# One step of a hybrid layer: the HGRN2 heads run inside the z phase, the gate product in the output stage

## The chip, the cores and the metric

The kernel runs on one core of a Trainium2 chip. The metric is device microseconds of one execution. Engines are named as in the profile: PE is TensorE (PEld its weight loads), DVE VectorE, ACT ScalarE, POOL GpSimd, SP the engine that issues most loads.

## What is computed

One layer of a streaming encoder on 512 prompt frames and 32 sample frames, which share all weights (T = 544 columns, kept transposed: channels on partitions).

```python
mod = silu(c) @ w_ada + b_ada                     # shift, scale, gate
h = rmsnorm(x) * (1 + scale) + shift
z = h @ w_in                                      # 2048 x 15360
au, av, ag, lx, lg, hq, hf, hi, hg, mg = split(z)
ya = gelu(au) * spatial_mix(rmsnorm(gelu(av))) * silu(ag)      # gMLP, 8 groups
yb = rglru(causal_conv(lx)) * silu(lg)                         # RG-LRU, 8 blocks
yc = rmsnorm(hgrn2(silu(hq), hf, hi)) * silu(hg)               # HGRN2, 8 heads
ga, gb, gc = split(sigmoid(mg))
out = (ga * (ya @ wb0) + gb * (yb @ wb1) + gc * (yc @ wb2)) @ w_out
y = rmsnorm(x + gate * out)
```

HGRN2 is a gated recurrence, worked out per head in chunks of 64 with decay factors for blocks of 1, 2, 4, 8, 16, 32 frames.

## The kernel before

Each large product is taken in about full fp32 precision as three reduced ones: a weight tile is split on chip into a rounded part `wh` (ACT copy) and a rest `wl` (DVE subtraction), in `split` and `halved`, and `rows3` multiplies `wh` with both parts of the operand and `wl` with the first.

The program is one list of *items* (`items`), each with a `prep` (split the weights of this item), a `mul` (its products) and a `post` (evict). The loop at the end emits, for item i: the loads that are due, `prep` of item i+2 (`AHEAD = 2`), `mul` of i, `post` of i, and one call of `pump()`. This emission order is the order of every engine's queue; an engine never passes a waiting instruction. Four stages follow each other:

- *Start*: 64 items that make shift and scale, beside the norm of x.
- *z phase*: 60 groups (`Group`), each makes two blocks of 128 channels of z with a Strassen-like scheme of 7 items; an item is 24 products of 128x128 by 128x272. Per group four weight tiles go through the ring `raw` (`RAWS` buffers of 512 KB) and one through the ring `q`; one of the `raw` tiles and the `q` tile get a second tile added in flight, by an accumulating DMA that POOL issues once the first has landed (`load_adds`, L267). `z_groups` sets the order of the groups: 4 of `av`, the light ones (heads' inputs hf, hq, hi, hg and the merge gates mg, whose results are spilled to DRAM), the 16 heavy ones (gMLP and RG-LRU) with light ones between. The small work of a gMLP group or an RG-LRU block is a generator (`gm_gen`, `lru_gen`) that `pump` advances by one step per item.
- *Merges*: `ya @ wb0` and `yb @ wb1` (16 blocks each of 48 products), then `yc @ wb2` in two passes of 16 half blocks (`part`). While they run, `pump` advances the 8 head generators (`hg_gen`), two at a time in turn, also between the parts of an item (`cuts`). The operands of the z phase are closed by then, and heads live in an arena of their own (`harena`, 46 units).
- *Output*: 16 blocks of `w_out` (two items of 48 products each), the residual and the last norm.

The gate product (`gate_item`, 32 items of 4 products whose stationary operand has 2 columns, through the ring `raw`) is spread over z groups 5 to 12, four to a group.

Of the kernel before, what the change touches and what calls it, by code (L numbers as in the profile page):

```python
# [13 lines left out]
NP = 512  # L14
# [28 lines left out]
RAWS = 6  # L43
# [63 lines left out]
def hybrid_step_kernel(ctx: ExitStack, tc: tile.TileContext, xT, cT, w_first, w_in, w_branch, w_out,  # L107
# [56 lines left out]

    arenas = {}
# [4 lines left out]
    def hbuf(n=T):  # L170
        try:
            return Buf(arenas["h"], n)
        except MemoryError:
            return Buf(arenas["a"], n)
# [134 lines left out]
    def halved(src, width=1024):  # L309

        wh = wp.tile([128, 1024], F32R, tag="wh", name="wh", bufs=3)
        wl = wp.tile([128, 1024], F32R, tag="wl", name="wl", bufs=3)
        split(wh[:, :width], wl[:, :width], src[:, :width])
        return wh, wl

    def rows3(p, w, rhs, kt, start, stop, **kw):

        wh, wl = w
        n = len(kt)
        for i, k in enumerate(kt):  # L320
            s = slice(i * 128, (i + 1) * 128)
            for q, (a, r) in enumerate(((wh, 0), (wh, 1), (wl, 0))):
                mm(p, a[:, s], rhs(k, r), start=start and i == 0 and q == 0,  # L323
                   stop=stop and i == n - 1 and q == 2, **kw)
# [78 lines left out]
    def plain_item(src, kt, rhs, p, first, last, post=None, pre=None, hs=(0, 1), cuts=(4,)):  # L403
# [8 lines left out]
        def mul():  # L412
            w = c.pop("w")
            n = len(kt)
            for lo, hi in zip((0, *cuts), (*cuts, n)):
                for h in hs:
                    rows3(pms[p][:, h, :HF], [a[:, lo * 128:hi * 128] for a in w], lambda k, r: rhs(k, r, h), kt[lo:hi],
# [14 lines left out]
    MIX = ((6, 5), (7, 3))  # L432

    def o_block(j, post, pre, hs):
        p = turn["p"] % 2
        turn["p"] += 1
        for z in range(2):
            plain_item(w_out[j, :, 8 * z:8 * z + 8, :].rearrange("p k n -> p (k n)"), range(8),
                       lambda k, r, h, z=z: X[MIX[z][h]][:, k, r, :], p, z == 0, z == 1,
                       (lambda: post(pms[p])) if z else None, None if z else pre, hs)  # L440

# [6 lines left out]
    heads = {"next": 8, "run": []}  # L448

    def pump():  # L450
# [39 lines left out]
    def square_x(q):  # L490
        if q == 0:
            st["xss"] = po()
        act(st["sq"][q % 2], st["x"][q], AF.Square)

    def sum_x(q):
        for i in range(2):
            for h in range(2):
                mm(st["xss"][:, 512 * h:512 * h + HF], ones, st["sq"][q % 2][:, i, h * HF:(h + 1) * HF],
                   start=q == 0 and i == 0, stop=q == 7 and i == 1)

    def rstd_x():
# [36 lines left out]
    def sums(c):  # L538
# [15 lines left out]
        put(4, c, hi)  # L554

    def start_items():
        for c in range(8):
            for part in range(2):
                for q in range(4):
# [18 lines left out]
                    def post(c=c, n=n):  # L578
# [13 lines left out]
                        if n == 3 and c == 4:  # L592
                            pools.close("early")
                            pools.close("scratch")
                            operand(pools.open("x4", "right"), 4)
                        if n == 7:
                            ada_post(c)
                            if c == 7:
# [5 lines left out]
                                operand(pools.open("x3", "right"), 3)  # L604
                                for i in range(4, 8):
                                    put(3, i, st["x"][i][:, :, :HF])
# [6 lines left out]
    NUNIT = 27  # L613
# [91 lines left out]
    def hg_setup():  # L705

        hg["x"] = hbuf(len(LEVELS) * XW)
# [3 lines left out]
        hg["A"] = [hbuf(SLOT) for _ in range(2)]  # L711
        for a in hg["A"]:
            nc.gpsimd.memset(a.ap, 0.0)
        t = hbuf(len(LEVELS) * 256)
        nc.gpsimd.dma_start(out=t.ap, in_=consts[:, 130:130 + len(LEVELS) * 256])
        nc.vector.tensor_copy(hg["masks"].rearrange("p a e n -> p (a e n)"), t.ap)
# [11 lines left out]
    def hg_gen(h):  # L728
        cell = {}
        zf, zi, zg = (hbuf() for _ in range(3))  # L730

        a = next(a for a in (arenas["h"], arenas["a"]) if a.pairs() > 1)
        kq = [Buf(a, T), Buf(a, T + 1)]
        kb, qb = sorted(kq, key=lambda b: b.col)
        kb.ap, qb.ap = kb.ap[:, :T], fv(qb.ap, 0, [[1, T + 1]])
        for b, n in ((zf.ap, "hf"), (qb.ap[:, 1:], "hq"), (zi.ap, "hi"), (zg.ap, "hg")):
            nc.gpsimd.dma_start(out=b, in_=scratch[f"{n} {h}"])
        nc.gpsimd.memset(qb.ap[:, 0:1], 0.0)
        if h == 0:
            hg_setup()  # L740
            for _ in range(3):
                yield
        yield
        lb, l1, ln1 = (lbt[:, i, h:h + 1] for i in range(1, 4))
        t1, t2, g = hbuf(), hbuf(), hbuf()
        act(t1.ap, zf.ap, AF.Abs)
        ts(g.ap, zf.ap, 0.0, None, op0=OP.min)
        act(t2.ap, zf.ap, AF.Relu)
# [13 lines left out]
        zf.free()  # L762
        cell.update(q=True, v=zi, hg=zg)
# [10 lines left out]

        def lev(m):
            if m not in LEVELS:
                return w32["b"].ap, 0
            i = LEVELS.index(m)
            return hg["x"].ap[:, i * XW:(i + 1) * XW], 128
# [29 lines left out]
        A = hg["A"][h % 2].ap  # L809
# [13 lines left out]
        def lev_put(m, p):  # L823
            i = LEVELS.index(m)
            for r, e, lo, n, half, src in ((128, 0, 0, 256, 1, 128), (128, 1, AO, 256, 0, 0),
# [3 lines left out]
                    o, hg["masks"][:r, i, e, :n // 2].rearrange("p (b m) -> p b m", m=m),  # L829
                    p[:r, src:src + n // 2].rearrange("p (b m) -> p b m", m=m))  # L830

        while "busy" in hg:
            yield
        hg["busy"] = h
# [3 lines left out]
        lev_w(1)  # L838
        lev_e(16)
        lev_e(8)  # L840
        lev_d(4)
        lev_d(2)
# [3 lines left out]
        p1 = lev_mm(1)  # L846
        lev_e(4)
        lev_e(2)
        lev_put(1, p1)
        lev_w(4)  # L850
        lev_w(2)
        lev_d(32)
# [5 lines left out]
        p1, p2 = lev_mm(16), lev_mm(8)  # L858
        lev_e(32)
        act(ke.ap, ke.ap, AF.Exp)  # L860
        eq, qe = hbuf(T + 1), hbuf(T + 1)
        nc.gpsimd.memset(eq.ap[:, 0:1], 0.0)
        act(eq.ap[:, 1:], g64.ap, AF.Exp)
        lev_put(16, p1)
        lev_put(8, p2)
# [10 lines left out]
        p1, p2 = lev_mm(4), lev_mm(2)  # L876
        mm(p1[:NS, 272:273], ke.ap[:, NP:], qb.ap[:, T:T + 1], start=True, stop=True)
        nc.vector.tensor_copy(A[:NS, AS + NS:AS + NS + 1], p1[:NS, 272:273])
        lev_put(4, p1)
        lev_put(2, p2)  # L880
        g32.free()
        g64.free()
        hg.pop("busy")
# [21 lines left out]
        for w in range(4):  # L905
            nc.tensor.transpose(pv[:, w * 128:(w + 1) * 128], cell["v"].ap[:, w * 128:(w + 1) * 128], ident)
# [14 lines left out]
        nc.tensor.transpose(pq[:NS, :128], cell["v"].ap[:, NP:], ident)  # L921
# [7 lines left out]
        cell["v"].free()  # L929
# [553 lines left out]
```

## Time and profile before

| | |
|---|---|
| median of 3 runs | 2284.67 us (2283.12 to 2287.73) |
| the profiled execution | 2280.29 us, span 2278.6 us |
| mean granted clock of PE | 0.953 |
| PE busy | 2058.2 us (90%), 15864 records |
| DVE, ACT, POOL busy | 1245.4, 995.2, 520.6 us |

The span is read by stages: start to 117.6 us, z phase to 1580 us, merges to 2070 us, output to 2262.5 us, and a tail to 2278.6 us. Within the z phase the gate items stand at 250 to 521 us, the gMLP groups mostly in 500 to 960 us, the RG-LRU blocks in 960 to 1580 us. PE, the engine with the most work, has matmuls that overlap each other, so its pace is read from how many of them a stretch holds. PEclk is the granted share of its full clock.

### The profile page before, as it was taken

What the parts mean: (1) busy time and instruction counts of PE and PEld (TensorE: products, weight loads), DVE (VectorE), ACT (ScalarE), POOL (GpSimd) and SP (SyncE); (2) the same over time, 40 slices, a digit from 0 to 9 for tenths busy, and PEclk for the clock granted to TensorE, in tenths of its full rate; (3) what the DMA queues carried; (4) which work ended last, traced back from release to release, by engine and by line L of the source; (5) the groups of instructions that cost most, each with busy time, mean ns of one, the idle gap of its engine ahead of it and who ended that gap; (6) DMA issues with size and microseconds to landing.
All of it is one profiled execution on the core that took longest, in us unless ns stands there. A gap on an engine that the chain in (4) does not pass through costs nothing. (4 is left out here: it accounts for less than half of the span.)

```text
span 2278.6 us, 39024 instructions
## 1 busy us (share of the span) xinstructions
PE 2058.2 (90%) x15864; PEld 1954.0 (86%) x15864; DVE 1245.4 (55%) x1729; ACT 995.2 (44%) x1616; POOL 520.6 (23%) x737
## 2 busy tenths in 40 slices
PE   5789878779999999999999999998798898979997
PEld 3279767669999999989999999998787888878997
DVE  3455434336666666566666666655655556443235
ACT  3455422224444444446464546544544444323233
POOL 0011110011121212111212111113645556322112
PEclk8789998899999999999999999999898999999999
DMA  8976575667677777766767676777343544765333
GB/s 326 374 186 173 163 205 175 181 201 207 186 208 190 194 199 199 195 165 174 191 168 194 174 188 180 201 197 236 128 148 115 146 121 111 183 207 172 113 113 125
DMA packets 139605, 416.57 MB, mean 183 GB/s; under 512 B 16641, under 2 KB 38945, under 8 KB 139425
## 3 DMA queue, kind: packets, MB, share of 16 engines
q1 hardware_dynamic: 89712, 261.08, 34.1%
q0 software_dynamic: 43728, 142.80, 27.8%
q10 hardware_dynamic: 5984, 10.19, 1.4%
q8 instruction: 125, 2.05, 0.4%
q14 instruction: 56, 0.45, 0.1%
HBM read 366.00 MB, written 48.01 MB: 182 GB/s over the span
## 5 line engine op out<-in xcount | busy, mean ns | idle before, releaser
L323 PE MATMUL pm<-x,wh 128*128 128x272 f32 x6720 | 1303.2, 293 | 72.3 <-ACT wh L188 48.7
L323 PEld LDWEIGHTS pm<-x,wh 128*128 128x128 f32 x6720 | 1081.0, 193 | 93.5 <-ACT wh L188 53.1
L323 PE MATMUL pm<-x,wl 128*128 128x272 f32 x3360 | 984.7, 293 | 6.7 <-DVE wl L233 6.7
L323 PEld LDWEIGHTS pm<-x,wl 128*128 128x128 f32 x3360 | 644.3, 192 | 11.3 <-DVE wl L233 11.1
L233 DVE TENSOR_TENSOR wl<-raw,wh 128x1024 fp32r<-128x1024 f32 (+1 forms) x342 | 408.1, 1194 | 330.0 <-ACT wh L188 329.2
L323 PE MATMUL pp<-x,wh 128*128 128x272 f32 x2048 | 415.2, 301 | 25.0 <-DVE arena L1205 23.2
L188 ACT ACTIVATE wh<-raw 128x1024 fp32r<-128x1024 f32 (+1 forms) x342 | 342.0, 1012 | 165.8 <-PE pm L323 88.3
L323 PEld LDWEIGHTS pp<-x,wh 128*128 128x128 f32 x2048 | 336.4, 198 | 32.6 <-issue 23.2
L233 DVE TENSOR_TENSOR wl<-q,wh 128x1024 fp32r<-128x1024 f32 x180 | 220.1, 1223 | 258.5 <-ACT wh L188 258.4
L323 PE MATMUL pp<-x,wl 128*128 128x272 f32 x1024 | 303.7, 297 | 1.1 <-DVE wl L233 1.1
L188 ACT ACTIVATE arena<-pm 128x272 f32<-128x272 f32 x240 | 94.5, 394 | 457.7 <-PE pm L323 446.1
L267 POOL DMA_DIRECT2D q<-in_w_in_dram x60 | 53.0, 883 | 737.6 <-DMA q<-in_w_in_dram 508.8
L188 ACT ACTIVATE wh<-q 128x1024 fp32r<-128x1024 f32 x180 | 189.3, 1052 | 66.9 <-DMA q<-in_w_in_dram 65.5
L323 PEld LDWEIGHTS pp<-x,wl 128*128 128x128 f32 x1024 | 201.5, 197 | 1.3 <-DVE wl L233 1.3
L188 ACT ACTIVATE arena<-arena 128x544 f32<-128x544 f32 (+3 forms) x166 | 90.6, 562 | 197.9 <-DVE arena L394 89.6
L364 DVE TENSOR_TENSOR q<-q,raw 128x1024 f32<-128x1024 f32 x120 | 147.1, 1226 | 4.1
L188 ACT ACTIVATE harena<-harena 128x272 f32<-128x272 f32 (+3 forms) x134 | 63.3, 532 | 74.1 <-DVE harena L766 21.7
L267 POOL DMA_DIRECT2D raw<-in_w_in_dram x60 | 54.1, 901 | 129.9 <-DMA raw<-in_w_in_dram 104.1
L1205 DVE TENSOR_TENSOR arena<-pp,arena 128x544 f32<-128x544 f32 x64 | 46.1, 720 | 50.7 <-DMA arena<-d_mg 27.7
L188 ACT ACT_TABLE_LOAD x44 | 56.5, 1283 | 13.6 <-DVE arena L1049 8.2
L791 POOL TENSOR_TENSOR harena<-harena 128x544 f32<-128x544 f32 (+1 forms) x39 | 54.7, 1424 | 1.4 <-DVE harena L806 1.3
L1209 POOL DMA_DIRECT2D d_mix<-arena x32 | 28.4, 888 | 91.2 <-DVE arena L1205 70.9
(332 smaller groups left out, 1785.2 us busy)
## 6 DMA issues: line engine op xcount, KB each, us to landing
raw<-in_w_in_dram SPq DMA_DIRECT2D x240, 512.0 KB, 5.5
q<-in_w_in_dram SPq DMA_DIRECT2D x60, 512.0 KB, 4.3
q<-in_w_in_dram POOLq DMA_DIRECT2D x60, 512.0 KB, 6.2
raw<-in_w_in_dram POOLq DMA_DIRECT2D x60, 512.0 KB, 7.4
raw<-in_w_ss_dram SPq DMA_DIRECT2D x44, 512.0 KB, 8.2
raw<-in_w_out_dram SPq DMA_DIRECT2D x38, 512.0 KB, 4.0
raw<-in_w_gate_dram SPq DMA_DIRECT2D x32, 512.0 KB, 5.4
raw<-in_w_branch_dram SPq DMA_DIRECT2D x32, 512.0 KB, 3.9
```

Of the source, the lines that this page charges most:

```text
L188: return nc.scalar.activation(out, in_, func, **kw)
L233: tt(lo, src, hi.bitcast(F32), op=OP.subtract)
L267: nc.gpsimd.dma_start(out=raws[n], in_=src, accum_op=OP.add)
L323: mm(p, a[:, s], rhs(k, r), start=start and i == 0 and q == 0, stop=stop and i == n - 1 and q == 2, **kw)
L364: tt(raws[n], raws[n], raws[m], op=OP.add)
L791: ptt(v, fv(src, 0, [[2 * m, nb], [m - 1, 2], [1, m]]), fv(src, m - 1, [[2 * m, nb], [0, 2], [0, m]]), op=OP.subtract)
L1205: tt(two(g.ap), halves(p), two(g.ap), op=OP.mult)
L1209: nc.gpsimd.dma_start(out=scratch[f"mix {j}"], in_=g.ap, accum_op=OP.add)
```

## The change

- *Heads in the z phase.* One head at a time, started when its four inputs are spilled (`heads["ready"]`); `pump` leaves out every third call for them. The order of groups is now 4 of `av`, then a head's group and a light one in turn (four groups and 28 items per head), 3 light, and the 16 heavy with one light one after every fourth. Heads use the common arena (32 units instead of 27, none of their own). The levels run in another order: 16 and 8 first, 1 last, with one step more between a level's factors and its products; only two factor buffers are kept, and `hi` and `hg` are loaded where they are used. The result is spilled (`y2`) and read back.
- *Smaller buffers.* `RAWS` is 5 instead of 6; `wh` and `wl` are five tiles of 512 instead of three of 1024, so each split is two instructions; PSUM has four banks `px` instead of two `px` and a pair `po`.
- *Gate product* in the output stage: 28 of its 32 items follow one `w_out` item each, the first four stand in the last merge.
- *Third branch* in one pass of 16 whole blocks; the mixed rows go to operands 1, 2, 6, 5. The convolution of RG-LRU has one step more.

```diff
@@ sizes and rings
-RAWS = 6
+RAWS = 5
-    NUNIT = 27
+    NUNIT = 32
-        return ps.tile([128, 512], F32, tag="x", name="px", bufs=2)
-    def po():
-        return ps.tile([128, 1024], F32, tag="o", name="po", bufs=1)
+        return ps.tile([128, 512], F32, tag="x", name="px", bufs=4)
@@ halved
-        wh = wp.tile([128, 1024], F32R, tag="wh", name="wh", bufs=3)
-        wl = wp.tile([128, 1024], F32R, tag="wl", name="wl", bufs=3)
-        split(wh[:, :width], wl[:, :width], src[:, :width])
-        return wh, wl
+        got = []
+        for o in range(0, width, 512):
+            wh = wp.tile([128, 512], F32R, tag="wh", name="wh", bufs=5)
+            wl = wp.tile([128, 512], F32R, tag="wl", name="wl", bufs=5)
+            split(wh, wl, src[:, o:o + 512])
+            got += [(wh[:, i:i + 128], wl[:, i:i + 128]) for i in range(0, 512, 128)]
+        return got
@@ pump
-        run = heads["run"]
-        while len(run) < 2 and heads["next"] < 8:
-            run.append(hg_gen(heads["next"]))
+        heads["tick"] += 1
+        if heads["tick"] % 3 == 0:
+            return
+        if heads["run"] is None and heads["next"] < heads["ready"]:
+            heads["run"] = hg_gen(heads["next"])
             heads["next"] += 1
-        if run:
-            g = run.pop(0)
-            if next(g, "end") != "end":
-                run.append(g)
+        if heads["run"] is not None and next(heads["run"], "end") == "end":
+            heads["run"] = None
@@ hg_gen
-        zf, zi, zg = (hbuf() for _ in range(3))
+        if h == 0:
+            hg_setup()
+        zf = hbuf()
...
-        while "busy" in hg:
-            yield
-        hg["busy"] = h
         lev_d(16)
         lev_d(8)
         yield
-        lev_w(1)
         lev_e(16)
         lev_e(8)
+        lev_w(16)
+        lev_w(8)
+        yield
+        p1, p2 = lev_mm(16), lev_mm(8)
+        yield
+        lev_put(16, p1)
+        lev_put(8, p2)
         lev_d(4)
         lev_d(2)
...
+        nc.gpsimd.dma_start(out=spill(f"y2 {h}"), in_=g)
@@ z_groups
-        todo += light[:10]
-        rest = iter(light[10:])
+        todo = av
+        for i in range(16):
+            todo += [head[i], light[i]]
+        todo += light[16:19]
+        rest = iter(light[19:])
         for i, (b1, b2, post, at_start) in enumerate(heavy):
             todo.append((b1, b2, post, {1: at_start}))
-            todo += [next(rest) for _ in range(1 + i % 2)]
+            if i % 4 == 3:
+                todo.append(next(rest))
...
-                if i in (2, 6, 5, 3) and 5 <= n < 13:
-                    gate_item(n - 5, (2, 6, 5, 3).index(i))
@@ merges
-        merge(1, 1, (6, 5), None, on1)
-        merge(2, 2, (1, 2), 0, wait(4))
-        merge(3, 2, (1, 2), 1, wait(9))
+        merge(1, 1, (6, 5))
+        merge(2, 2, (7, 3))
@@ out_items
+        def gate_next(j):
+            def f(z):
+                if j // 2 < 7:
+                    gate_item(j // 2 + 1, 2 * (j % 2) + z)
+            return f
-            o_block(j, post_j(j, (0, 1)), pre(j), (0, 1))
+            o_block(j, post_j(j, (0, 1)), pre(j), (0, 1), gate_next(j))
```

Three places of the engines' queues, before and after. The first is POOL in the z phase, between two groups that make head inputs; `raw` and `q` rows are the accumulating loads, `d_...` rows spills. Before:

```order
L1119 DMA d_hq_6_3661<-arena_820 128x544
L267 DMA raw_3566<-in_w_in_dram 128x1024
L267 DMA q_3701<-in_w_in_dram 128x1024
L1119 DMA d_hf_7_3912<-arena_820 128x544
L1119 DMA d_hq_7_3916<-arena_820 128x544
L267 DMA raw_3821<-in_w_in_dram 128x1024
L267 DMA q_3956<-in_w_in_dram 128x1024
```

After, where head 1 begins; L751 and L757 are the two sums of its gates, L765 and L788 the sums behind its scan and the factors of levels 16 and 8:

```order
L738 DMA arena_826<-d_hf_1_3401 128x544
L738 DMA arena_826<-d_hq_1_3405 128x544
L739 MEMSET arena_826 128x1
L751 TENSOR_TENSOR arena_826<-arena_826 128x544
L757 TENSOR_TENSOR arena_826<-arena_826 128x544
L765 TENSOR_TENSOR arena_826<-arena_826 128x8x32
L788 TENSOR_TENSOR arena_826<-arena_826 128x17x2x16
L788 TENSOR_TENSOR arena_826<-arena_826 128x34x2x8
L266 DMA raw_4087<-in_w_in_dram 128x1024
L266 DMA q_4202<-in_w_in_dram 128x1024
```

The two accumulating loads now stand behind eight instructions of a head.

The second is ACT at the gate step of a head (`hg_gen`, from Abs to the second Ln). Before, in the merges, the split in `wh` being that of one 48-product item:

```order
L188 ACTIVATE harena_15147<-harena_15147 128x34x8 x2
L188 ACTIVATE harena_15147<-harena_15147 128x544 x3
L188 ACTIVATE harena_15147<-harena_15147,cv_75 128x544
L188 ACTIVATE harena_15147<-harena_15147,lbt_80 128x544
L188 ACTIVATE harena_15147<-harena_15147 128x544
L188 ACTIVATE harena_15147<-harena_15147,lbt_80 128x544
L188 ACTIVATE wh_15386<-raw_14993 128x1024
```

After, in the z phase, `pm` rows being evictions of z items:

```order
L190 ACTIVATE wh_4078<-q_3926 128x512
L190 ACTIVATE wh_4082<-q_3926 128x512
L190 ACTIVATE arena_826<-pm0_115 128x272
L190 ACTIVATE arena_826<-arena_826 128x544 x2
L194 ACT_TABLE_LOAD
L190 ACTIVATE arena_826<-arena_826 128x544
L190 ACTIVATE arena_826<-arena_826,cv_75 128x544
L190 ACTIVATE arena_826<-arena_826,lbt_80 128x544
L190 ACTIVATE arena_826<-arena_826 128x544
L190 ACTIVATE arena_826<-arena_826,lbt_80 128x544
L190 ACTIVATE wh_4129<-raw_3849 128x512
L190 ACTIVATE wh_4133<-raw_3849 128x512
```

The step now holds a table load, and stands between the splits and evictions of items of 24 products.

The third is PE at a gate item. Before, between items 2 and 6 of a z group:

```order
L323 MATMUL pm0_114<-x2_69,wh_2078 128x272 x2
L323 MATMUL pm0_114<-x2_69,wl_2079 128x272
L1260 MATMUL px_2173<-raw_1845,cs_84 2x256 x4
L323 MATMUL pm1_115<-x6_68,wh_2139 128x272 x2
L323 MATMUL pm1_115<-x6_68,wl_2140 128x272
```

After, inside an output block, between its two items:

```order
L324 MATMUL pp0_18068<-x2_69,wh_21125 128x272 x2
L324 MATMUL pp0_18068<-x2_69,wl_21126 128x272
L1263 MATMUL px_21183<-raw_21047,cs_84 2x256 x4
L324 MATMUL pp0_18068<-x6_68,wh_21201 128x272 x2
L324 MATMUL pp0_18068<-x6_68,wl_21202 128x272
```

The item is the same four products; what stands around it has moved from `pm` to `pp`.

## Rows read from the trace of the kernel before

**Rows 1.** Stretches: busy us and records of each engine, PEclk, DMA share, GB/s.

```profile
250.00:500.00 250.00, 201.95 (x1535) 181.28 (x1534) 97.15 (x121) 69.39 (x98) 22.39 (x31) 0.90 0.65 187
500.00:960.00 460.00, 450.83 (x3550) 446.46 (x3549) 283.59 (x313) 214.53 (x276) 88.97 (x138) 0.99 0.73 199
960.00:1580.00 620.00, 595.99 (x4579) 588.55 (x4578) 399.45 (x488) 322.56 (x449) 110.04 (x188) 0.98 0.68 185
1580.00:2070.00 490.00, 424.06 (x3151) 396.36 (x3150) 267.29 (x527) 204.14 (x475) 241.71 (x316) 0.93 0.54 154
2070.00:2262.50 192.50, 191.44 (x1524) 191.06 (x1523) 70.56 (x95) 60.53 (x76) 32.89 (x28) 1.00 0.37 120
```

**Rows 2.** TensorE groups, 250 to 500 us: count, busy, mean ns, idle before.

```profile
L323 PE MATMUL pm<-x,wh 128*128 128x272 f32 x845 | 177.4, 309 | 36.1 <-ACT wh L188 36.1
L323 PE MATMUL pm<-x,wl 128*128 128x272 f32 x422 | 128.9, 305 | 3.1 <-DVE wl L233 3.1
L1260 PE MATMUL px<-raw,cs 128*2 128x256 f32 x240 | 18.4, 378 | 8.9 <-issue 7.7 <-DVE px L1256 1.2
```

**Rows 3.** ScalarE waits, 250 to 500 us: sum, times, longest.

```profile
ACT wh L188 <- DMA q<-in_w_in_dram: 50.2, 7, 8.2
```

**Rows 4.** TensorE in time order: one gate item.

```profile
384.73 0.61 PE L1260 MATMUL px<-raw,cs 128*2 128x256 f32 x8
```

**Rows 5.** GpSimd in time order, 389 to 402 us.

```profile
390.63 0.90 POOL L267 DMA_DIRECT2D raw<-in_w_in_dram  x1
401.15 0.88 POOL L267 DMA_DIRECT2D q<-in_w_in_dram  x1 [9.61 <-DMA q<-in_w_in_dram]
```

**Rows 6.** TensorE waits, 1580 to 2070 us.

```profile
PE pp L323 <- DVE arena L1205: 23.2, 18, 3.2
```

**Rows 7.** ScalarE in time order, gate step of one head, 1687 to 1696 us.

```profile
1687.72 1.75 ACT L188 ACTIVATE harena<-harena 128x544 f32<-128x544 f32 x3 [3.52 <-DMA harena<-d_hf]
1689.50 0.75 ACT L188 ACTIVATE harena<-harena,cv 128x544 f32<-128x544 f32 x1
1691.82 0.75 ACT L188 ACTIVATE harena<-harena,lbt 128x544 f32<-128x544 f32 x1 [1.57 <-DVE harena L754]
1693.53 0.66 ACT L188 ACTIVATE harena<-harena 128x544 f32<-128x544 f32 x1 [0.96 <-DVE harena L756]
1694.22 0.84 ACT L188 ACTIVATE harena<-harena,lbt 128x544 f32<-128x544 f32 x1
```

**Rows 8.** GpSimd in time order, same head.

```profile
1691.66 1.36 POOL L753 TENSOR_TENSOR arena<-arena,harena 128x544 f32<-128x544 f32 x1
1695.14 1.36 POOL L759 TENSOR_TENSOR arena<-arena,harena 128x544 f32<-128x544 f32 x1 [2.12 <-ACT harena L188]
...
1702.13 3.24 POOL L791 TENSOR_TENSOR harena<-harena 128x544 f32<-128x544 f32 x2
```

**Rows 9.** VectorE in time order, same stretch.

```profile
1696.04 1.54 DVE L233 TENSOR_TENSOR wl<-raw,wh 128x1024 fp32r<-128x1024 f32 x1 [2.55 <-ACT wh L188]
```

**Rows 10.** ScalarE splits by width, 1560 to 2280 us.

```profile
L188 ACT ACTIVATE wh<-raw 128x1024 fp32r<-128x1024 f32 x72 | 75.1, 1049 | 39.3 <-PE pp L323 39.2 <-ACT x3b L188 0.2
...
L188 ACT ACTIVATE wh<-raw 128x512 fp32r<-128x512 f32 x32 | 20.1, 628 | 31.7 <-PE pp L323 27.7 <-ACT x L188 2.3 <-ACT x3b L188 1.0
```

**Rows 11.** VectorE splits by width, 1560 to 2280 us.

```profile
L233 DVE TENSOR_TENSOR wl<-raw,wh 128x512 fp32r<-128x512 f32 x32 | 22.6, 706 | 6.4 <-ACT wh L188 6.4
```

**Rows 12.** Page, costliest groups, whole span.

```profile
L233 DVE TENSOR_TENSOR wl<-q,wh 128x1024 fp32r<-128x1024 f32 x180 | 220.1, 1223 | 258.5 <-ACT wh L188 258.4
...
L188 ACT ACT_TABLE_LOAD x44 | 56.5, 1283 | 13.6 <-DVE arena L1049 8.2
L791 POOL TENSOR_TENSOR harena<-harena 128x544 f32<-128x544 f32 (+1 forms) x39 | 54.7, 1424 | 1.4 <-DVE harena L806 1.3
```

**Rows 13.** TensorE waits, 960 to 1580 us.

```profile
PE pm L323 <- DVE arena L380: 15.0, 9, 1.8
```

**Rows 14.** ScalarE waits, 1580 to 1640 us.

```profile
ACT lbt L188 <- DVE lbt L720: 10.2, 1, 10.2
```

More of the change, by code (lines that the diff above doesn't have):

```diff
@@ L440, in o_block @@
                        (lambda: post(pms[p])) if z else None, None if z else pre, hs)
+            if between:
+                between(z)
     bg = []
@@ L445, in start @@
         bg.append(gen)
-    heads = {"next": 8, "run": []}
+    heads = {"next": 0, "ready": 0, "run": None, "tick": 0}
     def pump():
@@ L772, in hg_gen @@
         w32 = {}
+        xs = [hbuf(XW) for _ in range(2)]
         def lev(m):
@@ L875, in hg_gen @@
         yield
-        p1, p2 = lev_mm(4), lev_mm(2)
+        p1 = lev_mm(1)
         mm(p1[:NS, 272:273], ke.ap[:, NP:], qb.ap[:, T:T + 1], start=True, stop=True)
+        xs[0].free()
+        zi = hbuf()
+        nc.gpsimd.dma_start(out=zi.ap, in_=scratch[f"hi {h}"])
+        yield
         nc.vector.tensor_copy(A[:NS, AS + NS:AS + NS + 1], p1[:NS, 272:273])
[L879 to L883, printed above, removed]
+        lev_put(1, p1)
         yield
@@ L928, in hg_gen @@
         act(at.ap, pq[:, 256:], AF.Copy)
-        cell["v"].free()
+        zi.free()
         ke.free()
@@ L1058, in lru_gen @@
         yield
-        yield
-        ri = [[px(), px()], two(po())]
-        ri = [[x[:, :HF] for x in ri[0]], [ri[1][:, h, :HF] for h in range(2)]]
+        ri = [[px()[:, :HF] for _ in range(2)] for _ in range(2)]
         for n in range(2):
@@ L1102, in z_groups, with keep @@
     def z_groups():
-        todo = [(B_AV + j, B_AV + j + 1, av_post(j)) for j in range(0, 8, 2)]
-        def keep(*names):
+        av = [(B_AV + j, B_AV + j + 1, av_post(j)) for j in range(0, 8, 2)]
+        def keep(*names, on=None):
             def post(*os):
@@ L1120, in post, with on_head, f @@
                     o.free()
-            return post
-        light = [(B_HF + h, B_HQ + h, keep(f"hf {h}", f"hq {h}")) for h in range(8)]
-        light += [(B_HI + h, B_HG + h, keep(f"hi {h}", f"hg {h}")) for h in range(8)]
-        light += [(B_MG + j, B_MG + j + 1, keep(f"mg {j}", f"mg {j + 1}")) for j in range(0, 48, 2)]
+                if on:
+                    on()
+            return post
+        def on_head(h):
+            def f():
+                heads["ready"] = h + 1
+            return f
+        light = [(B_MG + j, B_MG + j + 1, keep(f"mg {j}", f"mg {j + 1}")) for j in range(0, 48, 2)]
+        head = []
+        for h in range(8):
+            head.append((B_HF + h, B_HQ + h, keep(f"hf {h}", f"hq {h}")))
+            head.append((B_HI + h, B_HG + h, keep(f"hi {h}", f"hg {h}", on=on_head(h))))
         heavy = []
@@ L1266, in mul @@
                 start(gate_sum(n, a))
-        item(None, mul)
+        item(prep, mul)
     def gate_sum(n, a):
@@ L1281, in on0 @@
                 open_pairs()
-                open_hgrn()
-                heads["next"] = 0
-            if j == 4:
+                open_tail()
                 start(y_gen(1, (6, 5)))
-        def on1(j):
-            if j == 0:
-                start(yc_gen())
-        def wait(n):
-            def on(j):
-                while j == 0 and ready.get("yc", 0) < n:
-                    pump()
-            return on
+            elif j == 10:
+                start(y_gen(2, (7, 3)))
         merge(0, 0, (1, 2), None, on0)
-        merge(1, 1, (6, 5), None, on1)
-        merge(2, 2, (1, 2), 0, wait(4))
-        merge(3, 2, (1, 2), 1, wait(9))
+        merge(1, 1, (6, 5))
+        merge(2, 2, (7, 3))
     ys, sumsq = {}, {}
@@ L1399, in hybrid_step_kernel @@
             pump()
-        while bg or heads["run"]:
+        while bg:
             pump()
-        for name in list(pools.open_):
+        for name in reversed(list(pools.open_)):
             pools.close(name)
```

169 lines of the change are left out of this document (79 added, 90 removed).

## The prediction

> **What bounds the kernel now.** I read the stretches first, then in each the groups and waits of PE. In the output stage PE is busy 191.4 of 192.5 us at full clock, for 1536 products (16 blocks of 96): 125 ns each [rows 1]. That is the price of a 128x272 product where nothing is in its way, so an item of the z phase costs 24 x 0.125 = 3.0 us and a merge block of 48 costs 6.0 us. Held against it, two stretches lose much.
>
> From 250 to 500 us, where the gate items stand, 845 + 422 = 1267 products are recorded [rows 2], worth 158 us; the stretch takes 250, so 92 us are over. PE is idle for 48 of them (250 - 202), and the clock, 0.90, takes 0.10 x 250 = 25 [rows 1]. The other 19 are the gate products: 30 items (240 records of 8 each) of 0.61 us [rows 2, 4]. So a gate item is cheap by itself, and dear through what it holds up: 36.1 of the idle us are PE waiting for `wh` [rows 2], and ACT in turn waits 50.2 us, seven times, up to 8.2 us, for a tile in the ring `q` [rows 3]. POOL shows why: it sits 9.61 us until the `q` tile has landed before it can issue the second, accumulating load [rows 5], and one `q` tile takes two loads in a row. With gate weights in SP's queue and in the ring `raw` both come too late.
>
> The merges, 1580 to 2070 us, hold 48 x 48 products = 288 us, and take 490. Of the 202 over, 490 - 424 = 66 are idle PE, 0.07 x 490 = 34 are the clock, 0.93 [rows 1]; 102 are left for the products of the eight heads (60 per head). Of the idle time 23.2 us are waits for DVE's merge product L1205 [rows 6], the other 43 lie with the heads.
>
> The 460 us from 500 to 960, z items with the gMLP work beside them, lose 9 us to idle PE and 5 to the clock of 0.99; 960 to 1580, with the RG-LRU blocks, lose 24 and 12 [rows 1]. So small work of other engines can be hidden in the z phase almost whole. In all three disturbed stretches the clock takes about half of what the idle time takes (25 beside 48, 34 beside 66, 12 beside 24), which I use below.
>
> **The change, part by part,** against the profiled span of 2278.6 us.
>
> *Gate items leave the z phase.* 92 us over in 250 to 500 fall to what 500 to 960 keeps, 14 in 460 us, so 5 in 158: -87. Two more gate items stand behind 500 us; with 92/30 = 3 us each, that is -93. I take -90. If the late `q` tile had other causes, only 30 x 0.61 = 18 us would go.
>
> *Gate items enter the output.* 28 x 0.61 = 17 us, and 3 us for the matmuls beside them, so +20. The output's load on DMA is 0.37, against 0.65 in the old place [rows 1], and no accumulating load hangs there. From above: 3 us each, as they cost in the z phase, or 84.
>
> *Merges.* 288 us of products, 4 gate items (2.4), and a rest: L1205's 23.2 us of waits came in 64 blocks, half of them 3 us long, with POOL, which fetches the gates, busy 242 of 490 us, mostly with heads [rows 1]. In 48 blocks of 6 us I take half, 12, and 4 for the clock: 306 instead of 490, -184. With no rest -200, with twice the rest -168.
>
> *Head products in the z phase:* +100, since all 102 are still issued, and the z phase has no idle PE to put them in.
>
> *New waits in the z phase.* This is the term that no row shows directly. (a) Gate step. ACT takes 1687.72 to 1695.06, 7.3 us, including waits of 1.57 and 0.96 for DVE and POOL's sum [rows 7, 8]. In the z phase a table load comes in (1.28 us, mean 1283 ns [rows 12]), because the sigmoids of the groups alternate with it: 8.6 us. Behind it on ACT wait the split of the next item but two (0.63 us [rows 10]) and the evictions, and PE waits for both. The splits run two items ahead: 12 us of cover in the merges, but 6.0 here. So 8.6 + 0.6 - 6.0 = 3.2 us per head, 26 in all. At least 0 if ACT is further ahead than that, at most 8.6 x 8 = 69. (b) The level steps, the state and the norm cost the heads 43 us in the merges. Here the first three products of a head have three items, 9 us, between them, the later ones 3 to 6: I take about half, 24; bounds 0 and, with half the cover, 86. (c) The first head's set-up, where ACT waited 10.2 us in one go [rows 14]: 6 of it come through the cover or the rest of the items (0 to 10). (d) The RG-LRU blocks now follow each other every 1.25 groups instead of 2.5, and PE already waited 15.0 us for DVE's eviction L380 there [rows 13]: as much again, 15 (0 to 30). (e) POOL's sums of a head, 1.36 to 1.6 us each [rows 8, 12], run beside DVE's splits. A split of 1024 that overlaps one took 1.54 us [rows 9], against a mean of 1223 ns in the z phase [rows 12], where POOL does little such work. With some three overlaps of 0.3 us per head on the path, 8 us.
>
> For (e) the Trainium skill has a harder rule ("SBUF — State Buffer", section "Who interferes with whom"): a DVE instruction with both inputs in SBUF and a GpSimd instruction that reads SBUF share a port, and the second fully blocks until the first is done. The trace agrees that they disturb each other (1.54 us for 1.22), and L1205, with one input in PSUM, is the kind the page exempts. What full blocking would do here is a rival below.
>
> Sum of the waits 26 + 24 + 6 + 15 + 8 = 79, and the clock half of that, 40: +119.
>
> *Splits in halves.* A pair of 512 takes 2 x 628 = 1256 ns on ACT, where one of 1024 takes 1049 [rows 10], and 2 x 706 on DVE [rows 11]: 0.2 us more per item on each. In the z phase ACT was busy 323 of 620 us and DVE 399 [rows 1], so this hides behind PE, except in (a) and (d), where it is in the margin I gave. RAWS 5 leaves 5/4 of a group between a load and its use, 26 us, where the gate stretch had 6/8, 18: nothing. The spill and reload of `y2` hide in the 0.73 DMA share of the z phase: nothing.
>
> Sum: 2278.6 - 90 + 20 - 184 + 100 + 119 = 2243.6 us, with the 1.7 us around the span 2245; the median of the runs shown lies 4.4 us above the profiled execution, so **2250 us**.
>
> **Rivals.** *Hidden heads.* The z phase takes the heads as it takes gMLP, whose 500 to 960 us lose little: waits of 25 instead of 79, the clock 13: 81 less, 2169 us. For it: ACT and DVE have a third to half of their time free there. Against it: the gate step is longer than the cover.
>
> *Late `q` tiles again (slower).* POOL's queue now has a head's sums, which wait for ACT and for the scan, ahead of the accumulating loads. From the start of the gate step to the last of these sums lie about 14 us (7.3 + 1.3 on ACT, then POOL's 1.36, the scan's 1.3 and 3.24 us of sums), and in the gate stretch a delay of this size cost (36.1 + 25)/8 = 7.6 us per group. If two of a head's four groups lose that, 16 x 7.6 = 122 us come on top: 2372. It decides from five groups on, since 35 us make up the whole forecast gain. For it: the accumulating load has no slack of its own, POOL waits for every `q` tile. Against it: PE itself is held by the same step, which gives the tile more time, and the tile is due some five items after POOL is asked for it.
>
> *Gate items stay dear.* In the output their weights share SP's queue and a ring of five with `w_out`; at the 3 us of the z phase they cost 84 instead of 20, 2314 us. Against it: half the DMA load.
>
> *Full port blocking.* POOL's sums of a head, some 11 of 1.4 us, hold off DVE or wait for it about half the time, 8 us per head instead of 1: 56 more and 28 of clock, 2334 us. This is what the rule of "SBUF — State Buffer" in the Trainium skill, named above, would make of it. Against it: the split of 1.54 us lost only 0.3.
>
> **How the numbers follow.** Forecast 0.58 (own range 2215 to 2295), hidden heads 0.15, late tiles 0.16, dear gates 0.05, blocking 0.06. Within 0.2%, 4.6 us either way, is no change for such a measurement. The forecast's own cases are faster for 0.50, same 0.05, slower 0.03; with the rivals faster 0.65, same 0.05, slower 0.30. For 8 in 10 the range runs from 2170 (hidden heads) to 2330, which takes in dear gates and part of the late tiles.
>
> **What would show it.** Gate stretch gone: no ACT waits on `q` tiles beyond a few us, and clock near 1.0, between 250 us and the first head. Merges: 300 to 312 us, idle PE under 20. Output plus tail: 225 to 235 us, and the gate records followed by a product within 0.7 us. z phase: 1580 to 1610 us, some 104 table loads (44 before), and the waits of PE on `wh` largest, once per head, at the gate step. Wrong if PE waits for `wh` with ACT waiting on `q` in most groups (late tiles), if idle PE in the z phase stays under 40 us (hidden heads), or if splits beside POOL's sums take over 2 us (blocking).

## The result and the profile after

The changed kernel takes 2248.89 us (median of 4 runs, 2244.99 to 2252.66) against 2284.1 us of before on the same chip: ratio 0.9843, 95% interval 0.9821 to 0.9865. The forecast was 2250 us. The profiled execution has a span of 2243.3 us.

First by stages, from the first product of each stage to that of the next, in us:

| stage | before | after | difference | forecast |
|---|---|---|---|---|
| start | 117.6 | 124.5 | +6.9 | 0 |
| z phase | 1463.7 | 1593.5 | +129.8 | +129 (-90 + 100 + 119) |
| merges | 485.5 | 290.7 | -194.8 | -184 |
| output | 195.7 | 218.7 | +23.0 | +20 |
| tail | 16.1 | 15.9 | -0.2 | 0 |
| span | 2278.6 | 2243.3 | -35.3 | -35 |

Stretches of the profile after: start and length, then busy us and records of PE, PEld, DVE, ACT, POOL, then PEclk, DMA share, GB/s. Heads' products stand at 335 to 1195 us, the RG-LRU's at 1454 to 1672.

```profile
124.50:300.00 175.50, 168.13 (x1298) 166.56 (x1299) 107.55 (x172) 105.83 (x248) 26.41 (x40) 0.97 0.68 183
300.00:1200.00 900.00, 818.52 (x6233) 789.14 (x6233) 572.02 (x964) 531.58 (x1034) 255.12 (x340) 0.95 0.61 168
1200.00:1440.00 240.00, 234.97 (x1848) 232.16 (x1848) 162.94 (x253) 135.47 (x227) 57.67 (x91) 1.00 0.73 190
1440.00:1718.00 278.00, 242.45 (x1715) 230.42 (x1714) 197.57 (x354) 168.24 (x297) 58.31 (x118) 0.93 0.57 152
1718.00:2009.00 291.00, 291.00 (x2338) 288.66 (x2339) 121.94 (x205) 80.96 (x159) 74.92 (x97) 1.00 0.69 202
```

Read against [rows 1]: the merges (last row), 66 us idle before, now have no idle time at full clock. The gate stretch with its clock of 0.90 is gone. The idle time is now in the heads' stretch, 900 - 818.5 = 81.5 us at a clock of 0.95, and with the RG-LRU, 35.6 us at 0.93; the gMLP's stretch keeps 5.0.

What PE waits for in the heads' stretch (sum, times, longest, us):

```profile
PE pm L324 <- DVE arena L381: 23.3, 7, 10.8
PE px L814 <- DVE arena L803: 17.5, 6, 5.9
PE pm L324 <- ACT arena L190: 14.0, 4, 7.3
PE pm L324 <- ACT wh L190: 13.1, 4, 4.6
PE px L878 <- DVE arena L868: 7.1, 3, 2.8
```

L381 and `arena L190` are evictions of z items, L803 and L868 the heads' own level steps. The longest wait, 10.8 us, is that of the one-time set-up at the first head. The four waits for `arena L190` and the four for `wh` are one per head, at its gate step: 2.3 to 4.6 us in seven heads, 7.3 in head 1, the worst, shown next. One gate step, head 1, on ACT in time order (start, duration, then the idle time before it in brackets):

```profile
425.42 1.21 ACT L190 ACTIVATE arena<-arena 128x544 f32<-128x544 f32 x2 [2.99 <-DMA arena<-d_hf]
426.64 1.28 ACT L194 ACT_TABLE_LOAD   x1
427.94 0.66 ACT L190 ACTIVATE arena<-arena 128x544 f32<-128x544 f32 x1
428.63 0.75 ACT L190 ACTIVATE arena<-arena,cv 128x544 f32<-128x544 f32 x1
430.17 0.75 ACT L190 ACTIVATE arena<-arena,lbt 128x544 f32<-128x544 f32 x1 [0.79 <-DVE arena L752]
431.83 0.66 ACT L190 ACTIVATE arena<-arena 128x544 f32<-128x544 f32 x1 [0.92 <-DVE arena L754]
432.52 0.84 ACT L190 ACTIVATE arena<-arena,lbt 128x544 f32<-128x544 f32 x1
433.27 1.13 ACT L190 ACTIVATE wh<-raw 128x512 fp32r<-128x512 f32 x2
434.31 0.37 ACT L190 ACTIVATE arena<-pm 128x272 f32<-128x272 f32 x1
```

It is [rows 7] in its new place: 425.42 to 433.27, 7.9 us, with the table load in it, and 2.99 us of waiting for the loaded hf ahead of it. Behind it stand a split and an eviction, and PE meanwhile:

```profile
427.19 0.29 PE L324 MATMUL pm<-x,wl 128*128 128x272 f32 x1
434.73 0.82 PE L324 MATMUL pm<-x,wh 128*128 128x272 f32 x2 [7.25 <-ACT arena L190]
```

PE stands still for 7.25 us until the eviction at 434.31 is done: it is short of a free PSUM bank, not of `wh`.

### The profile page after: what moved, and what is told of

It reads as the page before. It is cut to its first block, busy times and chain, and to the rows that moved or that the text cites. A ratio compares the mean times of both kernels' runs of the same rounds, so it can differ in the third digit from the quotient of the medians.

```text
span 2243.3 us, 40766 instructions
## 1 busy us (share of the span) xinstructions
PE 2052.4 (91%) x15864; PEld 1944.7 (87%) x15864; DVE 1292.6 (58%) x2204; ACT 1138.4 (51%) x2163; POOL 511.5 (23%) x720
## 3 DMA queue, kind: packets, MB, share of 16 engines
q1 hardware_dynamic: 87408, 261.08, 34.9%
## 4 chain that ended last, share of the span: by engine, by line
PE 55%; DVE 6%; issue 4%; ACT 3%; DMA 1%; POOL 1%; DVEq 0%; ACTq 0%; POOLq 0%
PE pm L324 29%; PE pp L324 22%; DVE wl L232 2%; ACT arena L190 1%; PE px L1067 1%; DVE q L365 1%; PE px L1263 1%; ACT wh L190 1%; PE px L814 1%; DVE arena L1052 0%; ACT L194 0%; DVE arena L381 0%; POOL arena L751 0%; DVE arena L395 0%; ACT L190 0%
## 5 line engine op out<-in xcount | busy, mean ns | idle before, releaser
L324 PEld LDWEIGHTS pm<-x,wh 128*128 128x128 f32 x6720 | 1087.2, 194 | 87.7 <-ACT wh L190 34.9
L232 DVE TENSOR_TENSOR wl<-raw,wh 128x512 fp32r<-128x512 f32 x652 | 466.4, 742 | 303.1 <-ACT wh L190 301.9
L190 ACT ACTIVATE wh<-raw 128x512 fp32r<-128x512 f32 x652 | 387.9, 624 | 326.8 <-PE pp L324 174.8
L324 PE MATMUL pp<-x,wh 128*128 128x272 f32 x2560 | 485.9, 289 | 0.6 <-DVE arena L395 0.6
L324 PEld LDWEIGHTS pp<-x,wh 128*128 128x128 f32 x2560 | 401.2, 189 | 14.9 <-issue 14.3
L324 PE MATMUL pp<-x,wl 128*128 128x272 f32 x1280 | 369.0, 288 | 0.0
L232 DVE TENSOR_TENSOR wl<-q,wh 128x512 fp32r<-128x512 f32 x360 | 252.5, 721 | 199.4 <-ACT wh L190 196.9
L190 ACT ACTIVATE wh<-q 128x512 fp32r<-128x512 f32 x360 | 218.0, 624 | 121.2 <-PE pm L324 94.5
L190 ACT ACTIVATE arena<-arena 128x544 f32<-128x544 f32 (+5 forms) x310 | 160.7, 554 | 195.4 <-DVE arena L1316 76.8
L190 ACT ACTIVATE arena<-pm 128x272 f32<-128x272 f32 x240 | 94.0, 392 | 163.4 <-PE pm L324 143.1
L788 POOL TENSOR_TENSOR arena<-arena 128x544 f32<-128x544 f32 (+1 forms) x40 | 53.5, 1359 | 57.1 <-PE px L816 30.0
L190 ACT ACTIVATE arena<-px 128x128 f32<-128x128 f32 (+4 forms) x136 | 43.1, 332 | 24.6 <-PE px L897 13.8
```

The source lines that it names most:

```text
L190: return nc.scalar.activation(out, in_, func, **kw)
L232: tt(lo, src, hi.bitcast(F32), op=OP.subtract)
L324: mm(p, a, rhs(k, r), start=start and i == 0 and q == 0, stop=stop and i == n - 1 and q == 2, **kw)
L788: ptt(v, fv(src, 0, [[2 * m, nb], [m - 1, 2], [1, m]]), fv(src, m - 1, [[2 * m, nb], [0, 2], [0, m]]), op=OP.subtract)
```

## The experiments

Each time is a median; intervals are of the ratio to before, run beside it. The changed kernel is "after", 2248.9 (0.9821 to 0.9865). e10, e12 and e13 ran on a chip where before takes 2281.1 us, so there the ratios compare better than the times.

**e1: the kernel before, only the gate items moved** (to the places they have in after).

```diff
-                if i in (2, 6, 5, 3) and 5 <= n < 13:
-                    gate_item(n - 5, (2, 6, 5, 3).index(i))
...
+            if n == 3 and j > 11:
+                gate_item(0, j - 12)
...
-            o_block(j, post_j(j, (0, 1)), pre(j), (0, 1))
+            o_block(j, post_j(j, (0, 1)), pre(j), (0, 1), gate_next(j))
```

> The kernel before with one part of the change alone: the 28 + 4 gate items go to the output stage and the last merge; heads stay in the merges, buffers as before. Theory: the gate items were dear only through the late q tiles, so this alone takes 90 us out of the z phase and puts 20 into the output: 2284 - 70 = 2214 us, below the changed kernel (2249), with ACT waiting on q tiles in the z phase for under 15 us instead of 65 and PE idle between 250 and 500 us under 10 instead of 48. Moving the heads was then a loss of some 35 us. Rival: the gain came from the heads leaving the merges, and gate items cost as much wherever they stand: 2275 to 2290 us.

2219.0 us, 0.9717 (0.9701 to 0.9733). The z phase falls by 99 us, the output grows to 221.5; the merges, with the heads still in them, grow by 14 us at a granted clock of 0.90 (0.93 before), for which no run gives the reason. The stretch of [rows 1, 3] now:

```profile
250.00:500.00 250.00, 249.58 (x1987) 249.23 (x1986) 154.69 (x162) 111.97 (x145) 42.21 (x63) 1.00 0.75 203
...
ACT wh L188 <- DMA q<-in_w_in_dram: 2.4, 3, 1.2
```

PE's 48 us of idle time there are 0.4, its records 1987 for 1535 (of which 240 were gate products), the clock 1.00, and ACT's waits for `q` 2.4 us for 50.2. So the gate product was what the late tiles came from (whether by the ring or by SP's queue was not tried apart), and its move alone is worth 65 us: more than the whole change. All the rest of the change together costs the other 30 (2248.9 - 2219.0; the forecast's terms for it, -184 + 100 + 119, give +35). That rest is the heads' move with the smaller buffers, the new order of groups, the four `px` banks and the single pass of the third branch; apart from the buffers (e3) these were not run one by one.

**e2: after, with the gate items back in the z phase** (the same lines the other way round).

> The changed kernel with its gate items put back into z groups 5 to 12, four to a group as before; heads in the z phase and small buffers stay. Theory: the late q tiles come back, 70 us or more, since heads and gate items now share the stretch and the ring has five buffers: 2249 + 70 = 2319 us (2305 to 2350), above the kernel before; ACT waits on q tiles over 40 us. Rival: the heads' waits there already give the tiles time, so gate items fit in: 2249 to 2265 us.

2290.62 us, 1.0029 (1.0017 to 1.0040): 42 us above after, between the two theories. ScalarE's waits from 124.5 to 1800 us, in e2:

```profile
ACT wh L190 <- DMA q<-in_w_in_dram: 70.4, 24, 9.5
ACT wh L190 <- DMA raw<-in_w_in_dram: 23.2, 7, 5.9
```

and in after:

```profile
ACT wh L190 <- DMA q<-in_w_in_dram: 25.4, 16, 2.9
...
ACT wh L190 <- DMA raw<-in_w_in_dram: 2.8, 1, 2.8
```

The late tiles come back with the gate items, and PE's waits for `wh` in the same stretch, first in e2, then in after, with them:

```profile
PE pm L324 <- ACT wh L190: 59.1, 14, 8.5
PE pm L324 <- ACT wh L190: 20.8, 7, 4.6
```

That they cost 42 us here and 65 in e1 fits that some of these waits now fall into time in which a head holds PE anyway; this was not measured by itself.

**e3: before, with RAWS 5 and the splits in halves.**

```diff
-RAWS = 6
+RAWS = 5
...
-        wh = wp.tile([128, 1024], F32R, tag="wh", name="wh", bufs=3)
...
+            wh = wp.tile([128, 512], F32R, tag="wh", name="wh", bufs=5)
```

> The kernel before with the smaller buffers alone: RAWS 5, and wh and wl as five tiles of 512 in place of three of 1024. Theory of the prediction: nothing, 2284 us within 0.3%, since ACT and DVE have room for 0.2 us more per item. Rival: with gate items in the ring of five, the q tiles come later still in the gate stretch, 8 groups by 2 to 5 us with the clock's half: 2305 to 2345 us, and the part of the smaller buffers in the change is a loss.

2279.57 us, 0.9984 (0.9972 to 0.9995): nothing, as forecast, in the sum. By stages its z phase is 8.5 us shorter and its merges 9.6 longer. And ACT's waits for `q` in the z phase double, here before and then e3:

```profile
ACT wh L188 <- DMA q<-in_w_in_dram: 65.5, 19, 8.2
ACT wh L188 <- DMA q<-in_w_in_dram: 128.2, 46, 8.2
```

PE's waits for `wh` do not follow (48.7 us, then 47.4). So waits of ACT for a tile show a loss only where PE waits behind them.

**e4: after, the gate step in two, the empty step behind the head's loads given up for it.**

```diff
         yield
-        yield
...
         act(t1.ap, zf.ap, AF.Abs)
+        act(t1.ap, t1.ap, AF.Exp, scale=-1.0)
+        act(t1.ap, t1.ap, AF.Ln, bias=cv[:, 1:2])
+        yield
...
         act(t2.ap, zf.ap, AF.Relu)
...
-        act(t1.ap, t1.ap, AF.Exp, scale=-1.0)
-        act(t1.ap, t1.ap, AF.Ln, bias=cv[:, 1:2])
```

> The changed kernel with the gate step of a head cut in two: Abs, Exp and the first Ln in one step, the rest in the next, and one of the two empty steps behind the loads of a head dropped. Theory: ACT's burst of 8 us against a cover of 6 is what PE waits for at the gate step (54 us of waits for wh and for evictions between 300 and 1200 us); cut into about 4 and 5 us it fits, so 25 to 40 of these us go and the clock's half of them: 2195 to 2225 us. Rival: PE waits there because POOL's sums and the accumulating loads behind them come late, which a cut does not change: 2240 to 2255 us.

2257.55 us, 0.9888 (0.9858 to 0.9919), no gain. Head 1 on ACT shows a flaw of the experiment:

```profile
421.75 0.66 ACT L190 ACTIVATE arena<-arena 128x544 f32<-128x544 f32 x1 [5.03 <-DMA arena<-d_hf]
```

A step earlier the head's input has not landed, and all of ACT's queue waits 5.03 us for it (17.9 us in all heads, 3.0 in after). So e4 does not settle it; e10 repeats it without this.

**e10: the same cut, the empty step kept**, and a step joined at the head's end.

```diff
         yield
         yield
...
         act(t1.ap, zf.ap, AF.Abs)
+        act(t1.ap, t1.ap, AF.Exp, scale=-1.0)
+        act(t1.ap, t1.ap, AF.Ln, bias=cv[:, 1:2])
+        yield
...
         nc.gpsimd.dma_start(out=S_new[1, h], in_=s0.ap[:, 128:])
-        yield
```

> The changed kernel with the gate step in two (as in e4), but with the empty step behind the head's loads kept, so that the first half does not wait for them, as it did in e4 (17.9 us of ScalarE waits for the loaded hf against 3.0 in the changed kernel); the number of steps is held by joining the state's spill and the transposes at the head's end. Theory (the length of ScalarE's burst sets the stall, and e4 lost its gain to the load): 2222-2236 us, and stalls of TensorE at a gate step sum to under 5 us a head. Rival (cutting divides the stall and does not shorten it, the last ScalarE operations waiting for the sums between them): 2243-2258 us.

2241.64 us, 0.9812 (0.9790 to 0.9835): 7 us under after, with a median inside neither range and an interval that overlaps that of after; its profiled span, 2241.7 us, is 1.6 under that of after. Its heads' stretch, and PE's waits there:

```profile
300.00:1200.00 900.00, 819.22 (x6236) 790.17 (x6235) 570.59 (x966) 538.35 (x1040) 252.99 (x340) 0.95 0.61 168
...
PE pm L324 <- DVE arena L381: 41.2, 10, 10.2
PE px L816 <- DVE arena L805: 14.0, 4, 5.2
PE px L993 <- DVE arena L978: 8.7, 4, 2.6
PE pm L324 <- ACT arena L190: 5.2, 3, 2.3
```

ACT's eviction falls from 14.0 to 5.2 us and `wh` from 13.1 to 0.6, and DVE's eviction L381 takes their place (41.2 for 23.3). The rival is nearer: PE is idle for 80.8 us of the stretch instead of 81.5, so the cut moves the stall and hardly shortens it. At head 6, where PE stands for 7.3 us, DVE's eviction stands in its queue behind an operation of the gate step that waits 1.22 us for POOL and a pair of splits that waits 2.11 us for ACT. The experiment is not quite clean, for the cut also brings six more table loads (110 for 104).

**e8: after, the heads' one-time set-up issued in the first head's own projection group.**

```diff
-        if h == 0:
-            hg_setup()
...
+        todo[4] += ({1: hg_setup},)
```

> The changed kernel with the heads' one-time set-up (mask, constants from HBM, table of lower bounds) issued in the first head's own projection group, some 100 us ahead of its first product, not at the first head's start. TensorE stands still for 11.1 us at 301.7 us there, with ScalarE waiting 12.3 us for VectorE, which waits 9.5 us for the constants' DMA. Theory (this stall is the set-up alone): it goes, and the time falls by 8 to 12 us, to 2237-2241 us. Rival (the first head's gate step takes its place, as the other heads' do): a gain of 3 us or less, 2246-2252 us.

2237.88 us, 0.9804 (0.9790 to 0.9818): 11 us, inside the theory's range. PE's waits at the first head, 10.9 us for the set-up and 2.3 at the gate step, become one of 5.9 at the gate step: the set-up's stall goes, as the theory says, and part of it comes back in the gate step, as the rival says.

**e5: after, the four light groups among the RG-LRU's blocks.**

```diff
-            if i % 4 == 3:
+            if i in (8, 10, 12, 14):
```

> The changed kernel with its four light groups placed behind blocks 0, 2, 4 and 6 of the RG-LRU, not behind every fourth heavy group. In the changed kernel TensorE is idle for 35.6 us of the 278 us from 1440 to 1718 us, at a granted clock of 0.93, and most of these waits are for the RG-LRU's steps on VectorE. Theory (the term for the RG-LRU was set too small, since consecutive blocks leave VectorE no time): idle there falls by 10 to 20 us and the time to 2230-2240 us. Rival (the blocks' own chain of steps holds TensorE, not their density; or the gMLP, which loses its two light groups, takes over the wait): 2245-2255 us.

2236.64 us, 0.9788 (0.9775 to 0.9801): 12 us, inside the theory's range. The stretch from 1440 to 1718 us in e5:

```profile
1440.00:1718.00 278.00, 255.65 (x1904) 247.58 (x1904) 200.87 (x332) 173.79 (x310) 64.19 (x124) 0.98 0.64 176
```

Idle time falls from 35.6 to 22.4 us, the clock rises from 0.93 to 0.98; in return the gMLP's stretch, 1200 to 1440, has 10.7 us idle instead of 5.0.

**e7: after, the gate step's two sums on DVE** instead of POOL.

```diff
-        ptt(g.ap, g.ap, t1.ap, op=OP.subtract)
+        tt(g.ap, g.ap, t1.ap, op=OP.subtract)
...
-        ptt(g.ap, g.ap, t1.ap, op=OP.add)
+        tt(g.ap, g.ap, t1.ap, op=OP.add)
```

> The changed kernel with the two sums of a head's gate step done on VectorE, not on GpSimd. In the first window of a head GpSimd's sums take 1.86 and 1.33 us, each hands over to another engine and back, and VectorE's splits beside them take 2.01 us a pair, not 1.29. Theory (the hand-overs to GpSimd lengthen the gate step, and every one of its microseconds is a stall of TensorE): each of 8 heads gains 1 to 2 us, 2233-2241 us. Rival (the stall is set by ScalarE's nine operations and the eviction queued behind them, e4 having shown that the size of the burst is not all): 2245-2253 us.

2244.37 us, 0.9825 (0.9811 to 0.9838): 4.5 us, just under the rival's range, and with an interval that overlaps that of after, so no gain is shown. The stall at head 1 goes from 7.3 to 6.4 us.

**e12: after, all of a head's sums and products of POOL on DVE** (every `ptt` in `hg_gen`, levels included).

```diff
-            ptt(v, fv(src, 0, [[2 * m, nb], [m - 1, 2], [1, m]]),
+            tt(v, fv(src, 0, [[2 * m, nb], [m - 1, 2], [1, m]]),
...
-        ptt(qe.ap, eq.ap, qb.ap, op=OP.mult)
+        tt(qe.ap, eq.ap, qb.ap, op=OP.mult)
```

> The changed kernel with all of a head's sums and products that GpSimd does (15 us a head) done on VectorE instead. In the changed kernel 82 weight splits on VectorE overlap such a GpSimd instruction and take 1263 ns on average, not 687, and those that start second end 0.55 us behind GpSimd's instruction whatever is left of it: 47 us of VectorE's time are held up. On VectorE the moved work takes about 60 us. Theory (the holding up reaches TensorE, as the rival of full blocking said): 2200-2230 us, splits back at 690 ns. Rival (it is mostly hidden, VectorE being busy 58% of the span, and the moved work costs as much as it frees): 2238-2256 us.

2235.54 us, 0.9797 (0.9781 to 0.9812): 13 us faster than after, or 10 by the ratios, just short of the rival's range and outside the theory's. What was held up can be seen in after, POOL and DVE from 439.3 us on:

```profile
439.39 1.14 POOL L788 TENSOR_TENSOR arena<-arena 128x544 f32<-128x544 f32 x1
439.76 1.32 DVE L232 TENSOR_TENSOR wl<-raw,wh 128x512 fp32r<-128x512 f32 x1 [1.08 <-ACT wh L190]
```

POOL's instruction ends at 440.53, the split at 441.08: 0.55 us later, though alone it takes 0.69. In after 35 splits start inside one such instruction of POOL and meet no second one; 34 of them end 0.55 to 0.58 us behind it, whether 0.11 or 1.32 us of it were left. The profile page's group of these splits, in after and in e12:

```profile
L232 DVE TENSOR_TENSOR wl<-raw,wh 128x512 fp32r<-128x512 f32 x652 | 466.4, 742 | 303.1 <-ACT wh L190 301.9
```

```profile
L232 DVE TENSOR_TENSOR wl<-raw,wh 128x512 fp32r<-128x512 f32 x652 | 437.7, 698 | 283.1 <-ACT wh L190 281.8
```

They take 742 ns with POOL beside them and 698 without most of it. So these sums of POOL and these splits of DVE do exclude each other. But of 47 us in which DVE is held up at most 10 to 13 reach the end, net of the work that DVE takes on, and the edit of e7 is part of that gain.

**e9: e5, e7 and e8 together; e13: with e12's edit as well** (the same lines).

> The changed kernel with the three edits together: light groups between the RG-LRU's blocks, the gate step's sums on VectorE, the set-up early. If each gains what its theory says, the sum of the gains is 25 to 45 us: 2205-2225 us, level with the kernel in which only the gate product moves (2219.0 us). If the rivals hold, 2240-2252 us.

> e9 (light groups between the RG-LRU's blocks, set-up early, the gate step's sums on VectorE) with the rest of a head's GpSimd sums on VectorE too. By the theory of e12 another 10 to 30 us on top of e9's 2216.2: 2186-2206 us. By its rival, level with e9: 2212-2222 us.

e9: 2216.21 us, 0.9702 (0.9689 to 0.9715); the single gains add up to 28 us and give 33. e13: 2214.73 us, 0.9709 (0.9691 to 0.9727), level with e9, as the rival of e12 had it: once the gate sums are on DVE and the other stalls repaired, moving the rest of POOL's sums brings nothing. Both are level with e1 (2219.0), which leaves the heads where they were: repaired, the heads' move costs about what it brings. These three are the fastest versions run.

## Why the prediction was right

*Gate items leave, -90.* e1 measured -99 for the z phase, and the cause was the one given: late `q` tiles behind gate weights. The split of the 92 us closed too well: 0.10 x 250 = 25 us counts the clock over idle time too. In the trace PE is busy for 35.7 us of that stretch at the lower clock, 1.2 GHz, and loses half of them, 18; so 26 us were left for the gate items, not 19. The -90 does not hang on this.

*Gate items enter the output, +20.* Measured +23.0, or 0.82 us per item; no product of `w_out` waits for its weights there.

*Merges, -184.* Measured -194.8. The step that failed is the rest: 12 us of waits and 4 of clock were kept from [rows 6], and none is left. Of these 23.2 us, 20.0 lie in 1970 to 2070 us of before, behind the last product of a head (1962.7 us). Their sum there, and one of them:

```profile
PE pp L323 <- DVE arena L1205: 20.0, 17, 2.2
...
2030.53 0.49 PE L323 MATMUL pp<-x,wh 128*128 128x272 f32 x2 [1.15 <-DVE arena L1205]
```

So they belong not to 64 blocks beside the heads but mostly to the last pass, whose half blocks have 24 products, 3 us, to hide an eviction: they follow each other every 4.4 us. After the change the third branch has whole blocks of 6 us, and no such wait. That the whole blocks are the reason fits this, but was not run by itself.

*Head products and new waits, +219.* Between e1 and after the z phase grows from 1364.7 to 1593.5 us, +229. The two z phases, e1 first:

```profile
117.00:1481.70 1364.70, 1323.34 (x10265) 1308.54 (x10265) 852.69 (x985) 681.29 (x980) 240.98 (x385) 0.98 0.70 189
...
124.50:1718.00 1593.50, 1464.07 (x11088) 1418.28 (x11089) 1040.09 (x1743) 941.12 (x1804) 397.51 (x586) 0.96 0.63 170
```

PE's idle time rises from 41 us to 129, so 88 for the 79 forecast. At the lower clock PE is busy for 38.0 us in e1 and 112.8 in after, and half of that is lost: +37 for the 40 forecast. That leaves 104 for the heads' products, forecast 100.

- (a), gate step: 26. Measured 27: 13.1 us for `wh` in four heads and 14.0 for an eviction by ACT in the other four, each behind the same step. The size was right. The sign, PE waiting for `wh` once per head, holds in half of the heads: the prediction saw that evictions wait behind the step too, but gave them no cover of their own and left them out of the sign. By e10 a shorter burst moves these waits to DVE's queue and does not remove them.
- (b), level steps, state and norm: 24. This was too small. The waits for L803 and L868 (24.6), for a loaded `hi` (2.0) and for the evictions L381 other than the set-up's (12.4) make 39.
- (c), set-up: 6. Measured 10.9, and e8 gains 11.
- (d), RG-LRU: 15. 35.6 us idle against 18.3 in the whole stretch from 960 to 1481.7 us in e1, so +17; e5, which spreads the blocks, takes 13 of the 35.6 out and gets 12 us back in the total, so the density was most of the reason.
- (e), POOL beside DVE: 8 us and 4 of clock. No wait of PE can be put down to it alone; e12 gains 10 to 13 us, e13 over e9 nothing, so its size stays open. The reason was wrong. The prediction read [rows 8, 9] as a split slowed by 0.3 us and held this against full blocking. The same rows say the opposite: POOL's sum ends at 1696.50, the split that began at 1696.04 ends at 1697.58, 1.08 us after it, and needs 1.22 alone [rows 12]. So of its work all but some 0.14 us came after the sum's end, as with the splits of 512 in after (0.55 us after it, 0.69 alone); it lost little only because it came late. The Trainium skill ("SBUF — State Buffer", "Who interferes with whom") calls the port that these two kinds of instruction share an exclusive lock, and the trace agrees with it, in 34 splits of 35. The sign that the prediction named, splits over 2 us, could not show it: the longest of the 35 took 1.95 us. The rival's price, 84 us, fell for another reason: PE waits only 4.8 us for `wl` in the whole z phase, so a held-up split rarely reaches it directly.

*The other rivals.* Late tiles: ACT waits 25.4 us for `q` tiles in the whole z phase, 2.9 at most, so POOL's longer queue costs little; e2 shows what it looks like when they are late. Hidden heads: refuted by 129 us of idle PE. Dear gates: refuted by the output's +23.

*Not in the sum:* the start is 6.9 us longer, at a clock of 0.70 from 60 to 120 us (0.76 before). e1 and e3 start in 117.0 and 119.1 us and every version with the heads moved in 122 to 125, so it goes with what they have and e1 and e3 have not; which part that is was not tried. It and the -11 of the merges, +3 of the output, +1 of the z phase cancel out: that the total is closer than its parts is luck.

## What to carry to other kernels

Price the two halves of a change apart: here the small half (128 products of a few columns, out of the way of loads that come in pairs) was worth 65 us, and the large half, moving heads out of a stage that idled, cost 30. What a head's chain held up moved along with it: 66 us of idle PE left the merges, some 46 of them from beside the heads, and 88 came to the z phase. When work with long chains goes beside dense items, count what covers an eviction (the banks, and the products of one item) as well as what covers a weight tile. And to tell blocking from slowing, compare the end of the late instruction with the end of the other one, not its duration with the mean.

## What the runs showed of the hardware

The clock around the 7.25 us stall in after (rows of the stall, of what follows it, and of the time after that):

```profile
427.48:434.70 7.22, 0.00 (x0) 0.00 (x0) 1.96 (x3) 5.43 (x10) 3.12 (x2) 0.65 0.00 0
434.70:442.00 7.30, 7.27 (x39) 7.13 (x39) 6.22 (x8) 3.54 (x8) 3.26 (x4) 0.64 0.45 144
442.00:450.00 8.00, 8.00 (x65) 7.70 (x64) 6.17 (x8) 6.31 (x11) 4.11 (x7) 1.00 0.83 135
```

The mean granted clock is 0.65 while PE stands still and 0.64 in the 7.3 us behind it. Both are mixes of its two levels, 1.2 and 2.4 GHz: the trace has the lower one from 429.7 to 439.9 us, so PE is busy again for 5.2 us before it rises. PE issues 39 products in that row instead of some 58. A stall of 7.2 us thus costs about 2.4 us more behind it (19 products of 0.125 us), since a low clock during the stall itself costs nothing.

That is a third of this one stall. Over all stalls it is more: in the heads' stretch PE is busy at the lower level for 69.8 us, which loses 34.9 beside 81.5 of idle time, 0.43 of it; in the whole z phase 56.4 beside 129.4, 0.44. The prediction's half was near.
